# Block 1's mixers: mLSTM decay rows as one product of both parts, scores in single-pass parts with two heads in turns, and k norms taken from the transposed k

## The chip, the cores and the metric

The kernel runs on one core of one Trainium2 chip. The metric is the device time of the program in microseconds (us), the median of several runs.

## The reference, cut to what matters

Two decoder blocks over 512 tokens of width 1024. Block 1 has two mixers side by side on the same normed input: a gated delta rule (GDN, 4 heads, head width 128) and an mLSTM (4 heads, query and key width 64, value width 128). The change touches two places of block 1.

```
qkv  = silu(causal_conv(concat[gq, gk, gv]))     # GDN inputs
k    = gk * rsqrt(sum(gk*gk, -1) + 1e-6)         # the k norm of each token and head
o_a  = gated_delta_rule(q, k, v, g, beta)

# mLSTM, here written over the whole sequence:
d_log[t, s] = b[t] - b[s] + i[s]   for s <= t, else -inf      # b: cumulative log forget gate
s[t, s]     = (q[t] . k[s]) * exp(d_log[t, s] - m[t])          # m: running maximum
num, den    = s @ v, sum(s, -1)
h           = num / max(|den|, exp(-m))
```

Then both mixers' outputs go through head norms, gates and projections; a feed-forward layer and a gate with `p` close block 1. Block 2 has a linear recurrence, a stick-breaking attention with 16 heads of width 64, and two feed-forward layers.

## The kernel before, in words

Everything is in fp32 of high accuracy. A weight matrix or an activation is held as two fp32r parts, `hi` (a rounded copy, written by ScalarE) and `lo` (what is left over, by VectorE: line 102 for weights), and a product is made of three single-pass matmuls (`mm3`, lines 173 to 175): low by high, high by low, high by high. A `slab` is one such projection of 128 output channels by 512 tokens: 24 matmuls of 128x512. It is a generator that yields after 6 matmuls; one such step is called a piece. `todo` holds the slabs of the projections that are still to come, `fill(n)` issues the next n pieces, and `after(n, fn)` has fn called n pieces later (`late`, `run_late`). TensorE's order is the order in which the code is written (`manual_schedule` for PE only); a planner orders the other engines' instructions at build time.

So in block 1 the small products of the two mixers are written between pieces of the large projections. The stretch that matters is the mLSTM loop, lines 586 to 612. For each head h and each 128-row block j of keys (w = 512, 384, 256, 128 query columns remain):

- `psS`: scores k.q, one matmul on fp32 tiles `mkT`, `mqT` (64 partitions: rows 0 to 63 for even heads, 64 to 127 for odd heads). The trace shows it as two instructions.
- `psr`: the row b[t] - m[t] of head h, spread over 128 partitions: two fp32r matmuls of 4 partitions (`sel` with `rjl`, then with `rjh`).
- ScalarE takes exp of `psr` into `D`, GpSimd cuts the triangle (`affine_select`), VectorE multiplies `psS` by `D` into `Sm` (line 601).
- `fill(2)`: two pieces.

After the four j of a head, `psn` (fp32, `Sm` by `mv`, line 608) is made in two groups, each followed by `fill(2)`. A loop over all heads has 48 pieces. `psS`, `psr`, `psn`, `pm` and others rotate in two PSUM banks with the tag "sa"; transposes use two with the tag "sb". The slabs that fill the loop are the 12 of GDN's q, k and v. When a slab ends, VectorE runs its convolution (`conv_silu`: six instructions of 128x512, lines 457 to 464), and six pieces later come its norm sums and transposes. For k that is `l2cols` (`pc`, line 474: four fp32 matmuls with a column of ones, eight instructions in the trace), a power -0.5 on GpSimd (line 203), the transpose `pk`, the multiply into `kn`, and two pieces later the transpose back (`pk2`).

Ahead of the loop, the tag "mvt" (two buffers) holds `zr` (gates, transposed by `pg`, line 391) and then the v projections on their way to their transposes (`pmv`, line 380). The rows are prepared in `rj` and split into `rjh` and `rjl`; `pm` and `enm` make exp(-m) by columns.

Of the kernel before, what the change touches and what calls it, by code (L numbers as in the profile page):

```python
# [9 lines left out]
F32 = mybir.dt.float32  # L10
F32R = mybir.dt.float32r
AF = mybir.ActivationFunctionType
# [41 lines left out]
def block_kernel(ctx: ExitStack, tc: tile.TileContext, xT, pT, cols, cst, wA, wBr, wO, w13, w2, wPG, wPL,  # L54
# [4 lines left out]
    def dump(name, aps):  # L59
        if dbg and name in dbg:  # L60
            for i, a in enumerate(aps):
                nc.sync.dma_start(dbg[name][i], a)
# [15 lines left out]
    def col(name, i=0, n=1):  # L78
        o, c = COFF[name]
        return COL[:, o + i:o + i + n]  # L80
# [115 lines left out]
    def bc_in(ap, n):  # L196
        return ap.unsqueeze(2).to_broadcast([ap.shape[0], ap.shape[1], n])
# [53 lines left out]
    def xtile(k):  # L251
        return xp.tile([P, T], F32, tag=f"x{k}", name=f"x{k}")
# [35 lines left out]
    with ExitStack() as ca:  # L288
# [3 lines left out]
        def pt(name, tag="sa", shape=(P, H, P)):  # L292

            return pps.tile(list(shape), F32, tag=tag, name=name)
# [15 lines left out]
        def after(n, fn):  # L310
            late.append((now[0] + n, fn))
# [9 lines left out]
        def fill(n):  # L321
            for _ in range(n):
                run_late(now[0])
                now[0] += 1
                while todo and next(todo[0], 1):
                    todo.pop(0)
# [15 lines left out]
        psq0 = gemm(pps, wA[O_MQ], A, tag="sb")  # L342
        R = norm_rows(pn, "nr", ss, "R0", rc0)
        LB = ca.enter_context(tc.tile_pool(name="LB", bufs=1, reuse_waits="tile"))
        o_b = LB.tile([P, H, T], F32, name="o_b")
        gz = LB.tile([P, H, T], F32, name="gz")
        cg = ExitStack()
        GP = cg.enter_context(tc.tile_pool(name="GP", bufs=1, reuse_waits="tile"))
# [11 lines left out]
        V.tensor_tensor(zr, psg, R, op=ALU.mult)  # L360
        V.tensor_scalar(zr, zr, col("gbias"), None, op0=ALU.add)

        mkT, mqT = [xtile(0), xtile(1)], [xtile(2), xtile(3)]
        for i in range(2):
            V.tensor_tensor(mkT[i], psk[i], R, op=ALU.mult)
        mv = ML.tile([P, NB, H, P + 1], F32, name="mv")
        G.memset(mv[:, :, :, P:P + 1], 1.0)

        def mq_done(i):
            return lambda ps: V.scalar_tensor_tensor(mqT[i], ps, 0.125, R, op0=ALU.mult, op1=ALU.mult)  # L370

        def mv_done(h):
            def f(ps):
# [77 lines left out]
        cwh = GP.tile([P, 48], F32, name="cwh")  # L451
        V.tensor_scalar(cwh, col("conv", 0, 48), 0.5, None, op0=ALU.mult)

        def conv_silu(ps, ti, out):
            cx = CV.tile([P, T + 3], F32, tag="cx", bufs=2, name="cx")
            G.memset(cx[:, 0:3], 0.0)
            V.tensor_tensor(cx[:, 3:], ps, R, op=ALU.mult)
            ac = CV.tile([P, T], F32, tag="ac", bufs=2, name="ac")
            V.tensor_scalar(ac, cx[:, 0:T], cwh[:, 4 * ti:4 * ti + 1], None, op0=ALU.mult)
            for j in range(1, 4):  # L460
                V.scalar_tensor_tensor(ac, cx[:, j:j + T], cwh[:, 4 * ti + j:4 * ti + j + 1], ac, op0=ALU.mult, op1=ALU.add)
            th = CV.tile([P, T], F32, tag="th", bufs=2, name="th")
            S.activation(th, ac, AF.Tanh)
            V.scalar_tensor_tensor(out, th, 1.0, ac, op0=ALU.add, op1=ALU.mult)

        def l2sq(src):
            sq = CV.tile([P, T], F32, tag="sq", bufs=2, name="sqk")
            S.activation(sq, src, AF.Square)
            return sq

        def l2cols(sq, which, h):
            pc = pn.tile([P, NB], F32, tag="nr", name="pc")
            for b in range(NB):
                TE.matmul(pc[:, b:b + 1], sq[:, b * P:(b + 1) * P], onec, start=True, stop=True)
            r = rqk[:, which, h, :]
            V.tensor_scalar(r, pc, EPS, None, op0=ALU.add)
            pw(r, r)
            return r

        def k_done(h):  # L480
            def f(ps):
                kt = CV.tile([P, T], F32, tag="cv", bufs=3, name="kt")
                conv_silu(ps, 3 * h, kt)
                sq = l2sq(kt)

                def g():
                    rk = l2cols(sq, 0, h)
                    pk = pt("pk", "sb")
                    for b in range(NB):
                        TE.transpose(pk[:, b, :], kt[:, b * P:(b + 1) * P], ident)  # L490
                    V.tensor_tensor(kn[:, :, h, :], pk, bc_in(rk, P), op=ALU.mult)
                    after(2, g2)

                def g2():
                    pk2 = pt("pk2", "sb")
                    for b in range(NB):
                        TE.transpose(pk2[:, b, :], kn[:, b, h, :], ident)
                    S.copy(knT[:, h, :], pk2.rearrange("p b t -> p (b t)"))
                after(LAG, g)
            return f  # L500
# [29 lines left out]
        def mo_done(h):  # L530
            def f(ps):
                assert ob_ready
                th = tp.tile([P, T], F32, tag="xin", bufs=3, name="tho")
                V.tensor_tensor(th, ps, R, op=ALU.mult)
                S.activation(th, th, AF.Tanh, scale=0.5)
                V.tensor_scalar(th, th, 0.5, 0.5, op0=ALU.mult, op1=ALU.add)
                V.tensor_tensor(o_b[:, h, :], o_b[:, h, :], th, op=ALU.mult)
            return f

        LAG = 6  # L540
# [19 lines left out]
        V.tensor_tensor_scan(mrow, rows[:, 0, :], rows[:, 1, :], 0.0, op0=ALU.add, op1=ALU.max)  # L560

        rj = ML.tile([H, 1280], F32, name="rj")
        ro = (0, 512, 896, 1152)
        for j in range(NB):
            V.tensor_tensor(rj[:, ro[j]:ro[j] + P], rows[:, 2, j * P:(j + 1) * P], mrow[:, j * P:(j + 1) * P],
# [2 lines left out]
            V.tensor_scalar(rj[:, ro[j] + P:ro[j + 1]], rj[:, ro[j + 1]:ro[j + 1] + T - (j + 1) * P],  # L568
                            rows[:, 2, (j + 1) * P - 1:(j + 1) * P], None, op0=ALU.add)
        fill(8)  # L570
        sel = ML.tile([H, H], F32R, name="sel")
        V.tensor_copy(sel, ident[0:H, 0:H])
        rjh = ML.tile([H, 1280], F32R, name="rjh")
        S.copy(rjh, rj)
        V.tensor_tensor(rj, rj, rjh.bitcast(F32), op=ALU.subtract)
        rjl = ML.tile([H, 3 * T], F32R, tag="rows", name="rjl")[:, 0:1280]
        V.tensor_copy(rjl, rj)
        pm = pt("pm", shape=(P, NB, H))
        for b in range(NB):
            TE.transpose(pm[:, b, :], mrow[:, b * P:(b + 1) * P], ident[0:H, 0:H])  # L580
# [2 lines left out]
        num = [xtile(4 + b).rearrange("p (h d) -> p h d", h=H) for b in range(NB)]  # L583
        den = ML.tile([P, NB, H], F32, name="den")
        msq = ML.tile([P, NB, H], F32, name="msq")
        for h in range(H):
            p0 = (h % 2) * 64
            Sm = ML.tile([P, 1280], F32, tag="Sm", bufs=1, name="Sm")
            for j in range(NB):
                w = T - j * P  # L590
                psS = pt("psS", shape=(P, T))
                TE.matmul(psS[:, 0:w], mkT[h // 2][p0:p0 + 64, j * P:(j + 1) * P], mqT[h // 2][p0:p0 + 64, j * P:],
                          start=True, stop=True)
                psr = pt("psr", shape=(P, T))
                for n, r_ in enumerate((rjl, rjh)):
                    TE.matmul(psr[:, 0:w], sel[:, h:h + 1].to_broadcast([H, P]), r_[:, ro[j]:ro[j] + w], start=(n == 0), stop=(n == 1))
                D = ML.tile([P, T], F32, tag="D", bufs=2, name="D")
                S.activation(D[:, 0:w], psr[:, 0:w], AF.Exp, bias=ccol[:, j, h:h + 1])
                G.affine_select(D[:, 0:P], D[:, 0:P], pattern=[[1, P]], base=0, channel_multiplier=-1,
                                compare_op=ALU.is_ge, fill=0.0)  # L600
                V.tensor_tensor(Sm[:, ro[j]:ro[j] + w], psS[:, 0:w], D[:, 0:w], op=ALU.mult)
                fill(2)
            for i2 in range(2):
                psn = pt("psn", shape=(P, 2, P + 1))
                for ii in range(2):
                    i = 2 * i2 + ii
                    for j in range(i + 1):
                        TE.matmul(psn[:, ii, :], Sm[:, ro[j] + (i - j) * P:ro[j] + (i - j + 1) * P], mv[:, j, h, :], start=(j == 0), stop=(j == i))
                for ii in range(2):
                    S.copy(num[2 * i2 + ii][:, h, :], psn[:, ii, 0:P])  # L610
                V.tensor_copy(den[:, 2 * i2:2 * i2 + 2, h:h + 1], psn[:, :, P:P + 1])
                fill(2)
        for b in range(NB):
            sqm = ML.tile([P, H, P], F32, tag="D", bufs=2, name="sqm")
            S.activation(sqm, num[b], AF.Square)
            V.tensor_reduce(msq[:, b], sqm, axis=AX.X, op=ALU.add)
        ad = ML.tile([P, NB, H], F32, name="ad")
# [10 lines left out]
        for b in range(NB):  # L628
            V.tensor_tensor(num[b], num[b], bc_in(mz.rearrange("p (b h) -> p b h", h=H)[:, b, :], P), op=ALU.mult)
        def ob_out():  # L630
            for h in range(H):
                po = pt("po", "sb")
                for b in range(NB):
                    TE.transpose(po[:, b, :], num[b][:, h, :], ident)
                S.activation(o_b[:, h, :], po.rearrange("p b t -> p (b t)"), AF.Copy, scale=col("mln", h))
            dump("o_b", [o_b[:, h, :] for h in range(H)])
            ob_ready.append(1)
        fill(LAG)
        run_late(1 << 30)
# [178 lines left out]
        BR = ca.enter_context(tc.tile_pool(name="BR", bufs=1, reuse_waits="tile"))  # L818
        oab = xset(BR, "o")
        for h in range(H):  # L820
            split(oab[4 + h], o_b[:, h, :])
        for h in range(H):
            V.tensor_tensor(oaT[:, h, :], oaT[:, h, :], gz[:, h, :], op=ALU.mult)
            split(oab[h], oaT[:, h, :])
# [579 lines left out]
```

## Time and profile before

| what | value |
|---|---|
| runs, median (lowest to highest) | 2080.22 us (2080.13 to 2083.77), 3 runs |
| the profiled execution's own time | 2082.17 us |
| its span, first to last instruction | 2080.2 us |
| TensorE busy | 2051.9 us, 99% |
| VectorE / ScalarE / GpSimd busy | 53% / 37% / 12% |
| mean granted TensorE clock | 0.995 |

The profiled execution's own time is 2.0 us longer than its span. A change in TensorE's time is to be read as start-to-start distances: matmuls are pipelined, so the durations of single ones overlap and add up to more than the time they take. The chain of waits adds up without overlap.

### The profile page before, as it was taken

What the parts mean: (1) busy time and instruction counts of PE and PEld (TensorE: products, weight loads), DVE (VectorE), ACT (ScalarE), POOL (GpSimd) and SP (SyncE); (2) the same over time, 40 slices, a digit from 0 to 9 for tenths busy, and PEclk for the clock granted to TensorE, in tenths of its full rate; (3) what the DMA queues carried; (4) which work ended last, traced back from release to release, by engine and by line L of the source; (5) the groups of instructions that cost most, each with busy time, mean ns of one, the idle gap of its engine ahead of it and who ended that gap; (6) DMA issues with size and microseconds to landing.
All of it is one profiled execution on the core that took longest, in us unless ns stands there. A gap on an engine that the chain in (4) does not pass through costs nothing.

```text
span 2080.2 us, 24373 instructions
## 1 busy us (share of the span) xinstructions
PE 2051.9 (99%) x9786; PEld 1705.2 (82%) x9786; DVE 1104.5 (53%) x1455; ACT 763.9 (37%) x1099; POOL 257.1 (12%) x266
## 2 busy tenths in 40 slices
PE   8999999999999999999899999999999999999998
PEld 7778899888888888887788888888888888888887
DVE  5667453554444423669964444333877754444322
ACT  4334232333232322546642323223555533322221
POOL 0111000131000000252320000001322220000011
PEclk9999999999999999999999999999999999999999
DMA  4211111343333333322323333333122123333332
GB/s 168 71 55 59 60 41 43 105 127 101 97 96 100 91 97 98 114 79 82 91 91 96 97 101 92 92 101 98 55 61 72 41 77 96 91 102 94 92 102 68
DMA packets 53664, 181.69 MB, mean 87 GB/s; under 512 B 5808, under 2 KB 7984, under 8 KB 53552
## 3 DMA queue, kind: packets, MB, share of 16 engines
q1 hardware_dynamic: 53408, 180.05, 28.9%
q8 instruction: 76, 1.25, 0.3%
q14 instruction: 36, 0.29, 0.0%
q10 hardware_dynamic: 144, 0.10, 0.0%
HBM read 178.03 MB, written 2.10 MB: 87 GB/s over the span
## 4 chain that ended last, share of the span: by engine, by line
PE 91%; DVE 5%; ACT 1%; issue 1%; POOL 1%; DMA 1%; SPq 0%; POOLq 0%; DVEq 0%; ACTq 0%
PE psmm L173 19%; PE psmm L174 19%; PE psmm L175 19%; PE psd L173 6%; PE psd L175 6%; PE psd L174 6%; PE z L1119 2%; PE po L1157 1%; DVE wlo L102 1%; PE pU L731 1%; PE pX L726 1%; PE t L1146 1%; DVE xc L987 1%; PE psv L173 1%; PE psv L174 1%
## 5 line engine op out<-in xcount | busy, mean ns | idle before, releaser
L101 ACT CAST whi<-raw 128x1024 fp32r<-128x1024 f32 (+1 forms) x333 | 344.5, 1036 | 942.3 <-issue 374.5
L102 DVE TENSOR_TENSOR wlo<-raw,whi 128x1024 fp32r<-128x1024 f32 (+1 forms) x333 | 411.0, 1235 | 287.9 <-ACT whi L101 287.8
L173 PE MATMUL psmm<-Bh,wlo 128*128 128x512 f32 x1032 | 402.3, 390 | 0.3 <-DVE Ol L1162 0.3
L174 PE MATMUL psmm<-Bl,whi 128*128 128x512 f32 x1032 | 402.2, 390 | 0.1
L175 PE MATMUL psmm<-Bh,whi 128*128 128x512 f32 x1032 | 402.1, 390 | 0.0
L173 PE MATMUL psmm<-Ah,wlo 128*128 128x512 f32 x832 | 332.9, 401 | 2.8 <-DVE wlo L102 1.9
L175 PE MATMUL psmm<-Ah,whi 128*128 128x512 f32 x832 | 325.2, 391 | 0.0
L174 PE MATMUL psmm<-Al,whi 128*128 128x512 f32 x832 | 324.4, 390 | 0.6 <-DVE Al L189 0.6
L173 PEld LDWEIGHTS psmm<-Bh,wlo 128*128 128x128 f32 x1032 | 193.8, 188 | 40.8 <-DVE Ol L1162 0.5
L175 PEld LDWEIGHTS psmm<-Bh,whi 128*128 128x128 f32 x1032 | 193.8, 188 | 40.3
L174 PEld LDWEIGHTS psmm<-Bl,whi 128*128 128x128 f32 x1032 | 193.8, 188 | 40.2 <-DVE Bl L189 0.5
L216 POOL TENSOR_TENSOR ss<-ss,sq 128x512 f32<-128x512 f32 x55 | 85.6, 1561 | 1141.7 <-issue 803.7
L173 PE MATMUL psd<-Hh,wlo 128*128 128x512 f32 x506 | 196.8, 389 | 0.0
L174 PE MATMUL psd<-Hl,whi 128*128 128x512 f32 x506 | 196.8, 389 | 0.0
L175 PE MATMUL psd<-Hh,whi 128*128 128x512 f32 x506 | 196.8, 389 | 0.0
L173 PEld LDWEIGHTS psmm<-Ah,wlo 128*128 128x128 f32 x832 | 156.3, 188 | 36.0 <-DVE wlo L102 3.2
L175 PEld LDWEIGHTS psmm<-Ah,whi 128*128 128x128 f32 x832 | 156.1, 188 | 33.6
L174 PEld LDWEIGHTS psmm<-Al,whi 128*128 128x128 f32 x832 | 156.6, 188 | 30.3 <-DVE Al L189 1.1
L870 DVE TENSOR_TENSOR u<-psmm,R 128x512 f32<-128x512 f32 x66 | 45.6, 691 | 194.2 <-PE psmm L175 194.2
L866 DVE TENSOR_TENSOR s<-psmm,R 128x512 f32<-128x512 f32 x66 | 45.7, 692 | 137.0 <-PE psmm L175 134.0
L175 PEld LDWEIGHTS psd<-Hh,whi 128*128 128x128 f32 x506 | 95.0, 188 | 19.8
L174 PEld LDWEIGHTS psd<-Hl,whi 128*128 128x128 f32 x506 | 95.0, 188 | 19.8
(468 smaller groups left out, 2475.9 us busy)
## 6 DMA issues: line engine op xcount, KB each, us to landing
raw<-in_f SPq DMA_DIRECT2D x120, 512.0 KB, 3.6
raw<-in_w SPq DMA_DIRECT2D x60, 512.0 KB, 3.5
raw<-in_wA SPq DMA_DIRECT2D x43, 512.0 KB, 3.5
raw<-in_bQKV SPq DMA_DIRECT2D x24, 512.0 KB, 3.5
raw<-in_aIn SPq DMA_DIRECT2D x16, 512.0 KB, 3.6
raw<-in_f SPq DMA_DIRECT2D x16, 384.0 KB, 3.1
x<-in_xT SPq DMA_DIRECT2D x16, 256.0 KB, 3.6
raw<-in_wBr SPq DMA_DIRECT2D x8, 512.0 KB, 3.5
```

The source lines that it names most:

```text
L101: copied[0] = S.copy(hi[:, :nk, :], raw[:, :nk, :])
L102: V.tensor_tensor(lo[:, :nk, :], raw[:, :nk, :], hi[:, :nk, :].bitcast(F32), op=ALU.subtract)
L173: TE.matmul(ps, l, xh, start=(first and i == 0), stop=False)
L174: TE.matmul(ps, h, xl, start=False, stop=False)
L175: TE.matmul(ps, h, xh, start=False, stop=(last and i == n - 1))
L216: eng.tensor_tensor(self.acc, self.acc, sq, op=ALU.add)
L726: heads(lambda h: TE.matmul(pX[:, h], Nm[:, h, :], odd(U)[:, h], start=True, stop=True))
L731: heads(lambda h: TE.matmul(pU[:, h], Tt[:, h, :], X[:, h], start=True, stop=True))
L866: V.tensor_tensor(s1, p1, R, op=ALU.mult)
L870: V.tensor_tensor(u, p3, R, op=ALU.mult)
L987: V.scalar_tensor_tensor(ac, cx[:, j:j + T], col("aconv", 4 * k + j), ac, op0=ALU.mult, op1=ALU.add)
L1119: TE.matmul(zs[g][:, o:o + w], qp[a][qs], kp[b][p0:p0 + 64, 0:w], start=(n == 0 and o == 0), stop=(n == 2), skip_group_check=True)
```

## The change

The mLSTM's k and q become pairs of parts (`mparts`: VectorE scales into a buffer of the tag "mvt", ScalarE and VectorE split it), the low parts in `mlo`, which shares its place with the later `o_b`. The rows' two parts are laid out in one tile `rjp`: partitions 0 to 3 and 64 to 67 hold the high parts, 32 to 35 and 96 to 99 the low parts, zeros elsewhere; `sel2` has the selecting ones at the same places. One matmul of 64 partitions then gives the sum of both parts. The loop goes over two pairs of heads: for each j first the two `psr` (rows 0 to 63 for the even head, 64 to 127 for the odd one), two pieces, then the scores as three single-pass matmuls for each head, the two heads in turns, and two pieces. exp writes straight into `Sm` (now two buffers). All `psn` of a pair follow. For k, `pc` is gone: ScalarE squares the transposed `pk` out of PSUM, VectorE reduces it, and the transpose back comes five pieces later instead of two. The three zeros ahead of each convolution are written once.

```diff
+        def mparts(k, src, c):
+            t = ML.tile([P, T], F32, tag="mvt", bufs=2, name="mkq")
+            V.scalar_tensor_tensor(t, src, c, R, op0=ALU.mult, op1=ALU.mult)
+            pair = xp.tile([P, T], F32R, tag=f"x{k}", name=f"mh{k}"), mlo[:, k, :]
+            split(pair, t)
+            return pair
...
-                sq = l2sq(kt)
                 def g():
-                    rk = l2cols(sq, 0, h)
                     pk = pt("pk", "sb")
                     for b in range(NB):
                         TE.transpose(pk[:, b, :], kt[:, b * P:(b + 1) * P], ident)
+                    sq = CV.tile([P, NB, P], F32, tag="sq", bufs=2, name="sqk")
+                    S.activation(sq, pk, AF.Square)
+                    rk = rqk[:, 0, h, :]
+                    V.tensor_reduce(rk, sq, axis=AX.X, op=ALU.add)
+                    V.tensor_scalar(rk, rk, EPS, None, op0=ALU.add)
+                    pw(rk, rk)
                     V.tensor_tensor(kn[:, :, h, :], pk, bc_in(rk, P), op=ALU.mult)
-                    after(2, g2)
+                    after(5, g2)
...
+        S.copy(rjp[0:H], rj)
+        rj2 = ML.tile([H, 3 * T], F32, tag="rows", name="rj2")[:, 0:1280]
+        V.tensor_tensor(rj2, rj, rjp[0:H].bitcast(F32), op=ALU.subtract)
+        S.copy(rjp[64:64 + H], rj)
+        for c in (32, 96):
+            V.tensor_copy(rjp[c:c + H], rj2)
...
-        for h in range(H):
-            for j in range(NB):
-                psS = pt("psS", shape=(P, T))
-                TE.matmul(psS[:, 0:w], mkT[h // 2][p0:p0 + 64, j * P:(j + 1) * P], mqT[h // 2][p0:p0 + 64, j * P:],
-                          start=True, stop=True)
-                psr = pt("psr", shape=(P, T))
-                for n, r_ in enumerate((rjl, rjh)):
-                    TE.matmul(psr[:, 0:w], sel[:, h:h + 1].to_broadcast([H, P]), r_[:, ro[j]:ro[j] + w], start=(n == 0), stop=(n == 1))
+        for hp in range(2):
+            for j in range(NB):
+                psr = [pt("psr", shape=(P, T)) for _ in range(2)]
+                for c, h in hc:
+                    p0 = 64 * c
+                    TE.matmul(psr[c][:, 0:w], sel2[p0:p0 + 64, h:h + 1].to_broadcast([64, P]),
+                              rjp[p0:p0 + 64, ro[j]:ro[j] + w], start=True, stop=True)
+                Ds = [Sms[h][:, ro[j]:ro[j] + w] for c, h in hc]
+                for c, h in hc:
+                    S.activation(Ds[c], psr[c][:, 0:w], AF.Exp, bias=ccol[:, j, h:h + 1])
+                    G.affine_select(Ds[c][:, 0:P], Ds[c][:, 0:P], pattern=[[1, P]], base=0, channel_multiplier=-1,
+                                    compare_op=ALU.is_ge, fill=0.0)
                 fill(2)
+                psS = [pt("psS", shape=(P, T)) for _ in range(2)]
+                for n, (a, b) in enumerate(((1, 0), (0, 1), (0, 0))):
+                    for c in range(2):
+                        p0 = 64 * c
+                        TE.matmul(psS[c][:, 0:w], kh[a][p0:p0 + 64, j * P:(j + 1) * P], qh[b][p0:p0 + 64, j * P:],
+                                  start=(n == 0), stop=(n == 2))
+                for c in range(2):
+                    V.tensor_tensor(Ds[c], psS[c][:, 0:w], Ds[c], op=ALU.mult)
+                fill(2)
...
-            sqm = ML.tile([P, H, P], F32, tag="D", bufs=2, name="sqm")
+            sqm = ML.tile([P, H, P], F32, tag="D", bufs=1, name="sqm")
```

## Rows read from the trace of the kernel before

**Rows 1.** The page: busy time (us, share, instructions), and the chain's shares.

```profile
PE 2051.9 (99%) x9786; PEld 1705.2 (82%) x9786; DVE 1104.5 (53%) x1455; ACT 763.9 (37%) x1099; POOL 257.1 (12%) x266
...
PE 91%; DVE 5%; ACT 1%; issue 1%; POOL 1%; DMA 1%; SPq 0%; POOLq 0%; DVEq 0%; ACTq 0%
```

**Rows 2.** Stretches: the mLSTM loop, 69 to 171 us: length, busy times, clock.

```profile
69.00:171.00 102.00, 102.00 (x501) 76.34 (x500) 69.71 (x115) 35.87 (x63) 17.51 (x33) 1.00 0.20 58
```

**Rows 3.** Chain of waits, 69 to 171 us: shares by line, pieces (start, length).

```profile
by line: PE psmm L173 22.0%; PE psmm L175 20.0%; PE psmm L174 20.0%; PE psS L592 11.5%; PE psr L596 7.7%; PE psn L608 7.2%; PE pc L474 6.2%; PE pk L490 1.9%; PE pv L517 1.7%; PE pk L497 1.6%; PE pm L580 0.3%
...
69.57 1.05 PE psS L592 x2
70.62 0.66 PE psr L596 x2
```

**Rows 4.** Chain of waits, 81 to 98 us.

```profile
82.31 0.23 PE psmm L175
82.54 0.41 PE psS L592 x2
82.95 0.36 PE psr L596 x2
83.32 0.98 PE pc L474 x8
...
93.02 0.79 PE pc L474 x8
...
96.64 1.05 PE psS L592 x2
```

**Rows 5.** Chain of waits, 1450 to 1456 us: block 2's scores of one head.

```profile
1451.23 2.12 PE z L1119 x12
1453.35 0.43 PE psmm L173
```

**Rows 6.** Timeline of TensorE there: start, duration, line, tile, shape.

```profile
1452.14 0.34 PE L1119 MATMUL z<-kh,ql 64*128 64x384 f32 x1
1452.32 0.34 PE L1119 MATMUL z<-kh,qh 64*128 64x384 f32 x1
...
1452.56 0.27 PE L1119 MATMUL z<-kh,ql 64*128 64x128 f32 x1
1452.67 0.27 PE L1119 MATMUL z<-kh,qh 64*128 64x128 f32 x1
...
1452.95 0.28 PE L1119 MATMUL z<-kh,ql 64*128 64x256 f32 x1
1453.08 0.28 PE L1119 MATMUL z<-kh,qh 64*128 64x256 f32 x1
```

**Rows 7.** Timeline of ScalarE as the loop begins (bracket: idle before, releaser).

```profile
69.31 1.04 ACT L101 CAST whi<-raw 128x1024 fp32r<-128x1024 f32 x1 [2.22 <-PE psmm L175]
70.27 0.18 ACT L582 ACTIVATE enm<-pm 128x16 f32<-128x16 f32 x1
71.32 0.69 ACT L598 ACTIVATE D<-psr,ccol 128x512 f32<-128x512 f32 x1 [0.87 <-PE psr L596]
...
76.13 0.63 ACT L468 ACTIVATE sqk<-kt 128x512 f32<-128x512 f32 x1
```

**Rows 8.** Timeline of VectorE, second head, first key block.

```profile
96.68 0.69 DVE L457 TENSOR_TENSOR cx<-psmm,R 128x512 f32<-128x512 f32 x1 [2.67 <-PE psmm L175]
...
99.88 0.69 DVE L601 TENSOR_TENSOR Sm<-psS,D 128x512 f32<-128x512 f32 x1 [0.19 <-POOL D L599]
100.49 1.53 DVE L461 SCALAR_TENSOR_TENSOR ac<-cx,cwh,ac 128x512 f32<-128x512 f32 x2
```

**Rows 9.** Timelines of VectorE and GpSimd after the loop.

```profile
167.08 1.38 POOL L203 TENSOR_TENSOR rqk<-rqk,mhalf 128x4 f32<-128x4 f32 x1 [0.48 <-DVE rqk L476]
...
177.28 0.63 DVE L616 TENSOR_REDUCE msq<-sqm 128x4 f32<-128x512 f32 x1
```

**Rows 10.** Chain of waits, 30 to 180 us: transposes ahead of the loop.

```profile
36.84 0.44 PE pg L391 x4
...
45.49 0.44 PE pmv L380 x4
```

More of the change, by code (lines that the diff above doesn't have):

```diff
@@ L344, in block_kernel @@
         LB = ca.enter_context(tc.tile_pool(name="LB", bufs=1, reuse_waits="tile"))
-        o_b = LB.tile([P, H, T], F32, name="o_b")
+        mlo = LB.tile([P, 4, T], F32R, tag="ob", name="mlo")
+        o_b = []
         gz = LB.tile([P, H, T], F32, name="gz")
@@ L361, in block_kernel @@
         V.tensor_scalar(zr, zr, col("gbias"), None, op0=ALU.add)
-        mkT, mqT = [xtile(0), xtile(1)], [xtile(2), xtile(3)]
-        for i in range(2):
-            V.tensor_tensor(mkT[i], psk[i], R, op=ALU.mult)
+        def mparts(k, src, c):
[4 more added lines that the diff above has]
+            return pair
+        mkT, mqT = [mparts(i, psk[i], 1.0) for i in range(2)], [None, None]
         mv = ML.tile([P, NB, H, P + 1], F32, name="mv")
@@ L369, in mq_done @@
         def mq_done(i):
-            return lambda ps: V.scalar_tensor_tensor(mqT[i], ps, 0.125, R, op0=ALU.mult, op1=ALU.mult)
+            return lambda ps: mqT.__setitem__(i, mparts(2 + i, ps, 0.125))
         def mv_done(h):
@@ L452, in block_kernel @@
         V.tensor_scalar(cwh, col("conv", 0, 48), 0.5, None, op0=ALU.mult)
+        cxs = [CV.tile([P, T + 3], F32, name=f"cx{i}") for i in range(2)]
+        for cx in cxs:
+            G.memset(cx[:, 0:3], 0.0)
         def conv_silu(ps, ti, out):
-            cx = CV.tile([P, T + 3], F32, tag="cx", bufs=2, name="cx")
-            G.memset(cx[:, 0:3], 0.0)
+            cx = cxs[ti % 2]
             V.tensor_tensor(cx[:, 3:], ps, R, op=ALU.mult)
@@ L536, in f @@
                 V.tensor_scalar(th, th, 0.5, 0.5, op0=ALU.mult, op1=ALU.add)
-                V.tensor_tensor(o_b[:, h, :], o_b[:, h, :], th, op=ALU.mult)
+                V.tensor_tensor(o_b[0][:, h, :], o_b[0][:, h, :], th, op=ALU.mult)
             return f
@@ L562, in block_kernel @@
         rj = ML.tile([H, 1280], F32, name="rj")
+        rjp = ML.tile([P, 1280], F32R, name="rjp")
+        G.memset(rjp.bitcast(F32), 0.0)
+        sel2 = ML.tile([P, H], F32R, name="sel2")
+        V.memset(sel2.bitcast(F32), 0.0)
+        for c in range(0, P, 32):
+            V.tensor_copy(sel2[c:c + H], ident[c:c + H, c:c + H])
         ro = (0, 512, 896, 1152)
@@ L570, in block_kernel @@
         fill(8)
[L571 to L577, printed above, removed]
+        S.copy(rjp[0:H], rj)
[4 more added lines that the diff above has]
+            V.tensor_copy(rjp[c:c + H], rj2)
         pm = pt("pm", shape=(P, NB, H))
@@ L585, in block_kernel @@
         msq = ML.tile([P, NB, H], F32, name="msq")
-        for h in range(H):
-            p0 = (h % 2) * 64
-            Sm = ML.tile([P, 1280], F32, tag="Sm", bufs=1, name="Sm")
+        Sms = [None] * H
+        for hp in range(2):
+            kh, qh = mkT[hp], mqT[hp]
+            hc = [(0, 2 * hp), (1, 2 * hp + 1)]
+            for c, h in hc:
+                Sms[h] = ML.tile([P, 1280], F32, tag="Sm", bufs=2, name="Sm")
             for j in range(NB):
                 w = T - j * P
-                psS = pt("psS", shape=(P, T))
-                TE.matmul(psS[:, 0:w], mkT[h // 2][p0:p0 + 64, j * P:(j + 1) * P], mqT[h // 2][p0:p0 + 64, j * P:],
-                          start=True, stop=True)
-                psr = pt("psr", shape=(P, T))
-                for n, r_ in enumerate((rjl, rjh)):
-                    TE.matmul(psr[:, 0:w], sel[:, h:h + 1].to_broadcast([H, P]), r_[:, ro[j]:ro[j] + w], start=(n == 0), stop=(n == 1))
[L597 to L601, printed above, removed]
-                fill(2)
[L603 to L611, printed above, removed]
-                fill(2)
@@ new lines, in block_kernel @@
+                psr = [pt("psr", shape=(P, T)) for _ in range(2)]
[4 more added lines that the diff above has]
+                Ds = [Sms[h][:, ro[j]:ro[j] + w] for c, h in hc]
+                for c, h in hc:
+                    S.activation(Ds[c], psr[c][:, 0:w], AF.Exp, bias=ccol[:, j, h:h + 1])
+                    G.affine_select(Ds[c][:, 0:P], Ds[c][:, 0:P], pattern=[[1, P]], base=0, channel_multiplier=-1,
+                                    compare_op=ALU.is_ge, fill=0.0)
@@ new lines, in block_kernel @@
+                fill(2)
+            for h in (2 * hp, 2 * hp + 1):
+                for i2 in range(2):
+                    psn = pt("psn", shape=(P, 2, P + 1))
+                    for ii in range(2):
+                        i = 2 * i2 + ii
+                        for j in range(i + 1):
+                            TE.matmul(psn[:, ii, :], Sms[h][:, ro[j] + (i - j) * P:ro[j] + (i - j + 1) * P], mv[:, j, h, :], start=(j == 0), stop=(j == i))
+                    for ii in range(2):
+                        S.copy(num[2 * i2 + ii][:, h, :], psn[:, ii, 0:P])
+                    V.tensor_copy(den[:, 2 * i2:2 * i2 + 2, h:h + 1], psn[:, :, P:P + 1])
+                    fill(2)
@@ L630, in ob_out @@
         def ob_out():
+            o_b.append(LB.tile([P, H, T], F32, tag="ob", name="o_b"))
             for h in range(H):
@@ L634, in ob_out @@
                     TE.transpose(po[:, b, :], num[b][:, h, :], ident)
-                S.activation(o_b[:, h, :], po.rearrange("p b t -> p (b t)"), AF.Copy, scale=col("mln", h))
-            dump("o_b", [o_b[:, h, :] for h in range(H)])
+                S.activation(o_b[0][:, h, :], po.rearrange("p b t -> p (b t)"), AF.Copy, scale=col("mln", h))
+            dump("o_b", [o_b[0][:, h, :] for h in range(H)])
             ob_ready.append(1)
@@ L820, in block_kernel @@
         for h in range(H):
-            split(oab[4 + h], o_b[:, h, :])
+            split(oab[4 + h], o_b[0][:, h, :])
         for h in range(H):
```

## The prediction

> **What bounds the kernel now.** I read the page first: TensorE is busy for 99% of the span and carries 91% of the chain that ended last, while no other engine is over 53% [rows 1]. So a microsecond taken from TensorE is a microsecond of the kernel, unless TensorE then has to wait. Next the stretches: in the mLSTM loop, 69 to 171 us, TensorE is busy for 102.00 of 102 us at the full granted clock, VectorE for 69.71, ScalarE for 35.87 and GpSimd for 17.51 [rows 2]. There is no gap to fill; only shorter TensorE work helps. Then the chain of waits, whose pieces add up without overlap: it tells what each small product costs between the large ones [rows 3, 4]. Last, block 2's scores, because they are what the new scores look like: 64 partitions, fp32r, three passes [rows 5, 6].
>
> **What leaves TensorE.** psS holds 11.5% of the 102 us, 11.7 us, and psr 7.7%, 7.9 us [rows 3]. The matmul behind such a group is also longer: the first large one after block 2's scores takes 0.43 instead of 0.23 us [rows 4, 5], and pc takes 0.98 behind a psr but 0.79 elsewhere [rows 4]. With 0.19 for each of the 16 groups that is 3.0 us more. Together 11.7 + 7.9 + 3.0 = 22.6 us for scores and rows. The four k norms lose their pc, at 0.79 each (the 0.19 is already counted): 3.2 us. psn, the transposes and the 48 pieces stay.
>
> **What comes in its place.** Every j of a pair of heads has one group of two psr and one of six score matmuls, so 2 x 4 x 2 = 16 groups again, and 2 x 4 x 8 = 64 single-pass matmuls. Their prices are in block 2. In a stream, one takes 0.18 us at 384 columns, 0.13 at 256 and 0.11 at 128, by the distances of the starts [rows 6], and 0.23 at 512, as the large ones do [rows 4]. Three of each are 1.95 us. The whole group, with what the next matmul loses, took 2.12 + 0.20 = 2.32 us [rows 5], so going into a group of 64 partitions and out again costs 0.37 us. Sixteen groups: 5.9 us.
>
> What no row shows is how two neighbours on different halves of the partitions go together. Both ends:
> - One after the other: 16 matmuls of each width, 16 x 0.65 = 10.4 us. With the 5.9, 16.3 us; 6.3 us saved.
> - Entirely side by side: half of it, 5.2 us, in all 11.1; 11.5 us saved.
>
> Between them: the 128-column step doesn't halve from 256 to 128 columns (0.13 to 0.11), so something that doesn't depend on the columns holds it; I take that to be the loading of its weights. If the columns of a pair run side by side but the two loads go in line, a pair takes 0.23, 0.22, 0.22 and 0.22 us, four pairs in each of eight j: 4 x 2 x 0.89 = 7.1 us, in all 13.0; 9.6 us saved. I take this. Block 2's matmuls can't overlap, since they share rows and accumulate in one bank; the new neighbours share neither. What speaks against it: psS of an odd head (rows 64 to 127) is as long ahead of its psr (rows 0 to 3) as that of an even head, 1.05 us both times [rows 3, 4], so different rows alone don't make those overlap. But those two have different sizes of row part, and a pair has the same.
>
> The Trainium skill (TensorE: Matmul & The Clock Gate, Part 3) says that matmuls on different row groups of the array run at the same time, a few ns apart; by it alone the saving would be near the 11.5 us, and no run here shows it yet.
>
> **Waits that come new.** The first psr now stands ahead of the first psS, and the pair wants both "sa" banks at once. One is held by pm until enm has read it, and enm stood behind a weight cast on ScalarE until 70.45 us [rows 7]. Before, psS ran meanwhile, from 69.57 to 70.62 [rows 3]; that cover is gone. The second psr could start near 69.9, so I price one wait at 0.6 us.
>
> In the loop each pair waits for the pair before it to leave the two banks, with 12 large matmuls, 12 x 0.23 = 2.8 us, as cover. The scores wait for two exps, 2 x 0.69 = 1.4 us, with a weight cast of 1.04 ahead of them [rows 7]: 2.4 us, which fits. The next psr wait for two multiplies, 2 x 0.69 = 1.4 us at 512 columns, behind the convolution that starts when a slab ends, that is, with the psr. It ran from 96.68 to 102.02 us, one multiply included [rows 8], so 4.7 us without it. The multiplies then end 4.7 + 1.4 = 6.1 us after psr began, and the next pair wants the banks after 0.5 (psr) + 2.8 + 0.9 (scores) + 2.8 = 7.0 us. It fits by 0.9 us, so nothing is charged. If another VectorE instruction of 0.69 or so is planned ahead of the multiplies, it still fits; with two, it doesn't. As the bound above I take 0.27 us at each of the 16 groups, 4.3 us: half of such a late instruction, less what is left of the cover.
>
> **Edits that I cost at nothing, and their cover.** The k norm's new line is Square 0.63 [rows 7], reduce 0.63, power 1.38 [rows 9] and multiply 0.69, some 3.5 us with the small add; five pieces are 5 x 6 x 0.23 = 6.9 us, so pk2 finds kn. With the old two pieces, 2.8 us, it would have waited about 0.7 us for each head. The splits of k and q (a scaling, a copy and a subtraction of about 0.7 us each, four times) pass through two "mvt" buffers, one of which zr keeps until pg, at 36.84. The next thing that TensorE wants from there is pmv at 45.49 [rows 10]: 8.6 us for three sequences of about 2 us. If this cover were short, pmv would wait, by about 1 us. The rows' layout adds a copy on ScalarE and a cast on VectorE ahead of the loop, where both have gaps. sqm has one buffer instead of two, and its squares and reductions take turns; the transposes that want the result come 11 pieces after the last psn, 15 us. The zeros of the convolution free GpSimd alone.
>
> **The sum.** 9.6 + 3.2 - 0.6 = 12.2 us. The profiled execution took 2082.17 us (span 2080.2), so 2070.0 for the like of it. The median of the runs, 2080.22, lies 1.95 below that execution, so 2068.0 us is the forecast.
>
> **Rivals.**
> - *In line:* the halves don't overlap. 6.3 + 3.2 - 0.6 = 8.9 us, 2071.3 us. For it: nothing in this trace shows two matmuls sharing time. Against: rows, banks and weights of the pair are apart.
> - *Banks:* the pairs double what must leave PSUM at once, and a group waits. With 0.27 us at each group on top of the forecast 2072.3 us, on top of the in-line case 2075.6. For it: VectorE is at 68% of the loop [rows 2] and gets a shorter loop with four more reductions. Against: the 0.9 us worked out above. The Trainium skill (TensorEngine Tiling (Array Packing), Performance Considerations, "PSUM Bottleneck") warns of just this: tiling makes TensorE faster, not the emptying of PSUM. By it the gain of the overlap could be lost here; in the trace of before VectorE's 69.71 us fit in 102.
> - *Slower:* the multiplies come so late that each of the eight psr pairs waits. At 2.05 us each, 16.4 us, the gain is gone and 4.2 us more: 2084.4 us. It decides when a whole convolution, 4.7 us, is planned between the scores and their multiplies, so that these end about 2.0 us after the 2.8 us of cover. Against: the multiply of before was let in between the convolution's instructions [rows 8].
> - *No change:* waits of about 12 us in all, or pieces that wait ahead of the loop: 2080 us.
>
> **How the numbers follow.** Chances: forecast (with full overlap at its lower end) 0.50, in line 0.25, banks 0.15, no change 0.06, slower 0.04. The range goes down to full overlap, 2066.1, less 1.6 if the second load of a pair covers 0.1 us of each group's entry: 2064.5. It goes up to in line with waits, 2075.5. That holds the first three cases but for their edges. A measurement here can tell about 0.2%, 4.2 us, from no change; the first three cases lie beyond it, but part of the third could end within: faster 0.88, same 0.08, slower 0.04.
>
> **What would show it.** In the chain of the profile after: psS and psr together, with the longer matmuls behind them, near 13 us in place of 22.6 (16 if in line); starts of the two psr of a pair under 0.2 us apart at 512 columns (0.3 if in line); k's pc gone, q's still there; one wait for enm, and none for D or Sm. The loop would last some 90 instead of 102 us. Wrong it would be if TensorE's waits list the multiplies or exps, or if a group costs much more than 0.37 us to enter and leave.

## The result, and the profile after

Four runs of each kernel, side by side: 2068.99 us median (2068.42 to 2071.58) against 2080.43 us (2080.13 to 2083.77). The ratio is 0.9944, 95% interval 0.9927 to 0.9961: 11.6 us faster, between 8 and 15. The forecast was 2068.0 us, with a range of 2064.5 to 2075.5. The profiled execution took 2071.58 us, with a span of 2069.8.

The page after, busy time, and the stretch of the loop (start and end, length, then busy time of TensorE, its weight loads, VectorE, ScalarE and GpSimd, clock, DMA):

```profile
PE 2037.0 (98%) x9754; PEld 1696.2 (82%) x9754; DVE 1110.8 (54%) x1468; ACT 766.6 (37%) x1104; POOL 261.2 (13%) x257
...
70.00:161.00 91.00, 88.33 (x467) 68.72 (x467) 70.82 (x117) 34.87 (x66) 18.55 (x22) 1.00 0.23 68
```

TensorE still bounds the kernel, but in the loop it is no longer busy throughout: 2.7 of the 91 us are idle, where there was none in [rows 2]. The chain of waits after, the second pair of heads at 512 and 384 columns and the first pair at 128:

```profile
119.91 0.42 PE psr L620 x2
120.33 0.43 PE psmm L173
...
123.28 0.89 PE psS L632 x6
127.53 0.37 PE psr L620 x2
...
130.83 0.72 PE psS L632 x6
```

```profile
95.56 0.26 PE psr L620 x2
95.82 0.43 PE psmm L173
...
98.81 0.48 PE psS L632 x6
```

They answer to [rows 3, 4]. Six score products of 512 columns take 0.89 us, less than the 1.05 of one fp32 product for one head before, and two psr take 0.42 instead of 0.66 for one. The 0.20 that the next matmul loses is as before.

TensorE's waits in the first 200 us (waiter, whom it waited for, total, times, longest):

```profile
PE psg L332 <- ACT whi L273: 5.4, 1, 5.4
PE pk L512 <- DVE kn L506: 2.2, 2, 1.1
PE prow L572 <- ACT rows L573: 0.8, 1, 0.8
PE psmm L173 <- DVE wlo L102: 0.7, 1, 0.7
PE psr L620 <- ACT enm L604: 0.5, 1, 0.5
PE po L670 <- ACT o_b L671: 0.5, 1, 0.5
```

psg, prow and po (0.3 us) waited before too. New are enm, 0.5 us, which was priced at 0.6, and kn, 2.2 us, which was priced at nothing: the transpose back of k found no kn for two of the four heads. The 0.7 us for a weight part (wlo) is new as well, but the control below doesn't have it.

From the end of pm to the end of the last psn, by TensorE's timeline, it was 69.57 to 175.49 us before and 70.56 to 164.59 after: 105.9 and 94.0 us, 11.9 less. The spans differ by 10.4, since the loop began 1.0 us later and some waits outside it differ by a microsecond or two (weight parts: 4.4 us in all against 2.5). The later start isn't the change's doing: in every other trace here pm begins 0.8 to 1.6 us later than in the one trace of before, also with the k norm alone (69.99 against 69.16 us), where TensorE's work ahead of the loop is that of before.

### The profile page after: what moved, and what is told of

Its sections match the earlier page's. It is cut to its first block, busy times and chain, and to the rows that moved or that the text cites. A ratio compares the mean times of both kernels' runs of the same rounds, so it can differ in the third digit from the quotient of the medians.

```text
span 2069.8 us, 24311 instructions
## 1 busy us (share of the span) xinstructions
PE 2037.0 (98%) x9754; PEld 1696.2 (82%) x9754; DVE 1110.8 (54%) x1468; ACT 766.6 (37%) x1104; POOL 261.2 (13%) x257
## 4 chain that ended last, share of the span: by engine, by line
PE 90%; DVE 5%; issue 1%; ACT 1%; POOL 1%; DMA 1%; SPq 0%; POOLq 0%; DVEq 0%; ACTq 0%
PE psmm L173 19%; PE psmm L174 19%; PE psmm L175 19%; PE psd L173 6%; PE psd L175 6%; PE psd L174 6%; PE z L1155 2%; PE po L1193 1%; DVE wlo L102 1%; PE pU L767 1%; PE pX L762 1%; PE t L1182 1%; DVE xc L1023 1%; PE psv L173 1%; PE psv L174 1%
```

## Experiments

Each ratio is to runs of the kernel before on the same chip and in the same job, five runs of each experiment unless said otherwise. Differences between experiments are differences of these ratios, with 0.0010 as 2.1 us. One ratio's interval reaches some 2.7 us to either side, a difference of two some 4 us, so for small differences the traces decide, and each experiment has one trace.

**The change again**, as a control beside the second set.

> The changed kernel itself once more, beside the three others of this job: 2069 us within the scatter, with the two waits for kn (2.2 us) and the one for enm (0.5 us) in the list again if they belong to the program and not to one execution.

Measured: 2069.74 us (2068.61 to 2071.39, 5 runs), ratio 0.9944 (0.9930 to 0.9958). kn 2.2 and enm 0.5 us are in the list again. The 0.7 us for a weight part is not: that one belonged to one execution. The profiled execution's span was 2067.0 us, 2.8 less than the first one's.

**Heads apart**: are the halves side by side at all? The comments in the cut sum up the lines that they stand for.

```diff
-        for hp in range(2):
+        for h in range(H):
+            hp, p0 = h // 2, 64 * (h % 2)
             for j in range(NB):
-                # two psr, fill(2), six score products in turns, two multiplies, fill(2)
+                # one psr, three score products (rows p0 to p0 + 63), one multiply, fill(2)
```

> The changed kernel with the heads one after another instead of in pairs: for each head and j one row product and three score products, all four on the same half of the partitions, then two pieces. As many groups (16) and as many matmuls (64), but no neighbour on the other half. Theory (the halves run side by side in the change): the 64 matmuls take 4 x 4 x 0.65 = 10.4 us plus 5.9 for going in and out, 16.3 us against about 11.1 in the change, so 5.2 us slower, 2074.2 us. Rival (order and pairing don't matter, single-pass parts give all): 2069.0 us.

Measured: 2071.97 us, ratio 0.9954 (0.9942 to 0.9967), 2.1 us slower than the change. Its chain, second head, 512 and 384 columns:

```profile
95.94 0.43 PE psr L616
96.37 0.69 PE psS L620 x3
...
100.02 0.37 PE psr L616
100.39 0.53 PE psS L620 x3
```

One psr for one head costs 0.43 us, as much as the two for a pair in the change; three score products cost 0.69 against six in 0.89, of which some 0.2 is the way in. Over all widths (psr 0.43, 0.37, 0.31, 0.26; scores 0.69, 0.53, 0.36, 0.33) four heads take 13.1 us; the change's two pairs take 2 x 4.00 = 8.0. So by the trace the pairs save 5.1 us of TensorE work, where the theory said 5.2, and "in line" is refuted. The time shows less, since in this order kn was never waited for (2.2 us back); a difference of 2.1 us alone would decide nothing.

**No turns**: does the order within the group matter?

```diff
                 for c, h in hc:
-                    p0 = 64 * c
+                    p0 = 0                    # both psr on the lower half
...
-                for n, (a, b) in enumerate(((1, 0), (0, 1), (0, 0))):
-                    for c in range(2):
+                for c in range(2):
+                    for n, (a, b) in enumerate(((1, 0), (0, 1), (0, 0))):
```

> The changed kernel with the pairs taken apart: both row products on the lower 64 partitions, and the three score products of one head before those of the other. Same instructions, same count. Theory (neighbours on different halves run side by side, loads included): each group of six scores keeps only one overlap, where one head follows the other, so it grows by two matmul steps, 0.46 us at 512 columns (0.89 to about 1.35 in the chain), and each pair of rows by one step (0.42 to about 0.65); 3 x 0.65 x 2 = 3.9 us in all, about 2072.9 us. Rival (halves never overlap, the saving is only that of single-pass parts and one row product): no change, 2069.0 us.

Measured: 2071.01 us, ratio 0.9952 (0.9940 to 0.9965), 1.7 us slower. The psr part came as expected, the scores did not. Timeline of TensorE and then the chain, 512 columns:

```profile
75.46 0.51 PE L632 MATMUL psS<-mh,mlo 64*128 64x512 f32 x2
75.80 0.41 PE L632 MATMUL psS<-mlo,mh 64*128 64x512 f32 x2
76.02 0.41 PE L632 MATMUL psS<-mh,mh 64*128 64x512 f32 x2
```

```profile
120.89 0.66 PE psr L620 x2
124.51 0.91 PE psS L632 x6
```

Two psr on one half take 0.66 instead of 0.42 us: one step of 0.23 more, so they go one after the other (0.54 for 0.37 at 384, 0.36 for 0.26 at 128). But the six scores, written as three of one head and then three of the other, still take 0.91 us, and the timeline shows them start two by two. The other head's first product, fourth in the code, started with the first. That the queue holds them in the order of the code, the semaphore counts in the trace bear out: in turns the last product of the second head adds a single count at each of the eight places, while here the last products of both heads add several at once. So what matters is that the group holds work for both halves; the turns themselves gave nothing. The theory's 1.3 us for psr was right, its 2.6 us for the scores wrong.

**The old k norm**, with the rest of the change.

```diff
+                sq = l2sq(kt)
...
+                    rk = l2cols(sq, 0, h)
...
-                    S.activation(sq, pk, AF.Square)
...
-                    V.tensor_reduce(rk, sq, axis=AX.X, op=ALU.add)
...
-                    after(5, g2)
+                    after(2, g2)
```

> The changed kernel with the k norm as before: squares from the untransposed k, four products with a column of ones, the transpose back two pieces later. Theory (the new k norm saves 3.2 us of TensorE work but made the transpose back wait twice for 1.1 us): those two waits go and 3.2 us of products come back, so about 1.0 us slower, 2070.0 us. Rival (the transposes' waits are only taken from a later wait): 3.2 us slower, 2072.2 us.

Measured: 2069.72 us, ratio 0.9945 (0.9932 to 0.9957): 0.2 us slower, which tells little by itself. No wait for kn is in its trace and no other has taken its place, so by the trace the new norm in this place was worth 3.2 - 2.2 = 1.0 us.

**The k norm alone**, put into the kernel before.

```diff
 # before.py
-                    rk = l2cols(sq, 0, h)
...
+                    S.activation(sq, pk, AF.Square)
...
+                    V.tensor_reduce(rk, sq, axis=AX.X, op=ALU.add)
...
-                    after(2, g2)
+                    after(5, g2)
```

> The kernel before with the new k norm alone (transpose back five pieces later), scores and rows as before. Theory: the products with ones are gone, 3.2 us, and the line of about 10 us finds five pieces and the groups between them, some 9 to 10 us: between no wait and 1.1 us for each head, so 2077.2 to 2081 us, nearer the lower end. Rival (the norm is worth its 3.2 us in full): 2077.2 us with no wait for kn.

Measured: 2076.89 us (9 runs), ratio 0.9980 (0.9971 to 0.9990), 4.2 us faster than before (2.1 to 6.0), and no wait for kn: the rival's case. So it is not the norm's line by itself that is too long for five pieces, but that line in the new order of the loop. The timelines of ScalarE and VectorE for the first head show another order on both engines: the Square stands ahead of the weight cast and the reduction ahead of the weight's low part.

```profile
86.41 0.58 ACT L490 ACTIVATE sqk<-pk 128x512 f32<-128x512 f32 x1
87.53 1.05 ACT L101 CAST whi<-raw 128x1024 fp32r<-128x1024 f32 x1 [0.54 <-PE psmm L175]
```

```profile
88.14 0.67 DVE L492 TENSOR_REDUCE rqk<-sqk 128x4 f32<-128x512 f32 x1
...
89.20 1.22 DVE L102 TENSOR_TENSOR wlo<-raw,whi 128x1024 fp32r<-128x1024 f32 x1
...
91.32 0.69 DVE L495 TENSOR_TENSOR kn<-pk,rqk 128x512 f32<-128x512 f32 x1 [0.17 <-POOL rqk L203]
```

From the end of pk's transposes (84.73) kn took 7.3 us here, and the transposes back came 2.6 us after it (94.57).

**Two pieces** instead of five.

```diff
-                    after(5, g2)
+                    after(2, g2)
```

> The changed kernel with k's transpose back two pieces after the norm, as before the change. Theory (the norm's line takes about 10 us): three pieces less are 4.1 us less cover; in the trace of the change two heads waited 1.1 us and the other two had about 2 us to spare, so the waits become 2 x 5.2 + 2 x 2.1 = 14.6 us instead of 2.2: 12.4 us slower, 2081.4 us. Rival (the prediction's 3.5 us line): a wait of 0.7 us for each head, 2.8 instead of 2.2, 2069.6 us.

Measured: 2099.05 us (4 runs), ratio 1.0084 (1.0070 to 1.0097), some 29 us slower than the change. The waits, the stretches behind each of the four (start and end, length, busy times, granted clock, DMA), and the chain behind the first wait:

```profile
PE pk L512 <- DVE kn L506: 22.4, 4, 6.5
```

```profile
93.12:96.20 3.08, 3.08 (x10) 2.60 (x11) 0.54 (x1) 0.59 (x1) 0.00 (x0) 0.50 0.00 0
123.50:126.92 3.42, 3.42 (x10) 2.63 (x9) 0.69 (x1) 1.10 (x2) 0.00 (x0) 0.50 0.03 13
154.95:161.05 6.10, 6.10 (x16) 4.52 (x16) 0.45 (x1) 0.59 (x1) 0.00 (x0) 0.50 0.00 0
186.37:191.77 5.40, 5.40 (x15) 4.43 (x16) 1.88 (x3) 1.10 (x2) 0.00 (x0) 0.50 0.04 17
```

```profile
93.12 1.11 PE pk L512 x4
94.24 0.43 PE psmm L173
...
95.94 0.41 PE psmm L174
96.35 0.23 PE psmm L175
```

All four heads waited, 22.4 us in all, 20.2 more than in the change. I had taken off 4.1 us of cover for the three pieces alone; but the small products between the pieces went with them, and by the timelines the cover fell from 9.1 to 3.1 us for the first head and from 9.9 to 3.5 for the second. The other 9 us are in the clock. TensorE waited 6.4, 4.6, 6.5 and 4.9 us, and then worked at half the full clock (0.50, that is 1.2 instead of 2.4 GHz) for 18.0 us in the four stretches together. The large matmuls take 0.43 us there, and are back at 0.23 from 96.35 on; an estimate from these numbers: at 0.23 for 0.43 the 18.0 us of work would take 8.4 us less, at double the clock 9.0. The rival, the 0.7 us for each head of the prediction, is refuted.

**Seven pieces.**

```diff
-                    after(5, g2)
+                    after(7, g2)
```

> The changed kernel with the transpose back of k seven pieces later instead of five. Theory (k's norm line needs about 10 us, since its Square is queued behind a weight cast and its reduction behind the convolution; two pieces are 2.8 us more): no wait of TensorE for kn, 2.2 us faster, 2066.8 us. Rival (the wait moves to the next user of the same PSUM banks or to the loop's end): no change, 2069.0 us.

Measured: 2066.34 us, ratio 0.9931 (0.9917 to 0.9944), 2.7 us faster than the change by the ratios, which is within their scatter of some 4 us; its slowest run, 2068.16, is below the change's fastest, 2068.42, but that ran in another job. The trace decides: no wait for kn is left, and it did not move elsewhere. Its chain also has the groups of 256 columns, which the change's chain leaves out:

```profile
133.88 0.31 PE psr L620 x2
137.16 0.55 PE psS L632 x6
```

**Seven pieces and two more covers.**

```diff
-                    after(5, g2)
+                    after(7, g2)
...
-            V.tensor_copy(sel2[c:c + H], ident[c:c + H, c:c + H])
+            G.tensor_copy(sel2[c:c + H], ident[c:c + H, c:c + H])
...
-        pm = pt("pm", shape=(P, NB, H))
+        pm = pt("pm", "sb", shape=(P, NB, H))
```

> As the one with seven pieces, and two more covers: the tile pm in the other pair of PSUM banks, so that the first pair of rows needn't wait for enm, and the four selecting copies on GpSimd instead of VectorE, where they stood ahead of a weight split at the kernel's start. Theory: 0.5 us and up to 0.7 us less than the seven pieces alone, about 2065.6 us, with neither wait in the list. Rival (these waits are of one execution only, or covered by others): 2066.8 us.

Measured: 2065.38 us (2064.35 to 2067.92), ratio 0.9925 (0.9913 to 0.9938): 4.0 us faster than the change and the fastest version here. The first psr now follow pm at once:

```profile
70.32 0.34 PE pm L602 x4
70.65 0.42 PE psr L620
```

enm is gone from the list. The step from the seven pieces, 1.2 us by the ratios, is smaller than the interval; by the trace 0.5 us of it are enm's. What the copies on GpSimd gave can't be told, since the weight wait that they were to remove was absent from the control as well.

## Why the prediction was right, and where it was right by chance

- *What bounds it, and what leaves TensorE.* Right. The kernel followed TensorE's work, and pc's 3.2 us came in full where nothing waited (the k norm alone: 4.2 us, interval 2.1 to 6.0).
- *Sixteen groups at 0.37 us for the way in and out.* Right. psr and psS take 2 x (0.42 + 0.37 + 0.31 + 0.26 + 0.89 + 0.72 + 0.55 + 0.48) = 8.0 us, with 16 x 0.19 behind them 11.0 us, 11.6 less than the 22.6 of before. The lower bound, everything side by side, was 11.1; the sign looked for was near 13.
- *The weight loads of a pair go in line.* This step failed: I took 7.1 us for the products where the bound below, 5.2, was the true one. At 128 columns the two psr take 0.26 us and three pairs of scores 0.48, so a further pair costs 0.11 us, what [rows 6] have for one matmul: the loads cost no more in a pair than alone. 13.0 - 11.0 = 2.0 us were missed here. The Trainium skill (TensorE: Matmul & The Clock Gate, Part 3) says that matmuls on different row groups run at the same time, and the trace agrees: six products in 0.89 us. It also says that matmuls start in the order of the program; what the last section reports differs from that.
- *In line.* Refuted by the heads apart: 13.1 against 8.0 us.
- *enm.* Right: 0.5 us for 0.6, and gone when pm has other banks.
- *Banks, and slower.* No wait for D, Sm or a bank of theirs in any trace of the change. The 0.9 us that were left held: for the second pair at 512 columns the multiplies ended 5.9 us after psr began (6.1 in the prediction), and the next psr came 7.6 us after it (7.0). The 0.27 us for each group doesn't follow from the prediction's own words, since one instruction of 0.69 fits into 0.9. The warning of the Trainium skill (TensorEngine Tiling (Array Packing), Performance Considerations), that tiling doesn't speed up the emptying of PSUM, did not come true for these banks; VectorE's two multiplies, which empty them, do stand in the k norm's line below, with 0.75 us.
- *The k norm at nothing, five pieces as cover.* This step failed, by 2.2 us. I added durations, 3.5 us, and left out what stands ahead of each on its engine; the line took 10.1 us for two heads and 8.0 and 8.3 for the others. The cover was misjudged too, the other way: 9.1 us instead of 6.9 for the first head (83.39 to 92.47), since two psr, six scores and q's pc stand between the five pieces. The chain of the change shows the line for the first head, from the end of pk's transposes at 83.39 us to the transposes back:

```profile
82.80 0.59 PE pk L499 x4
...
86.23 1.06 ACT whi L101
...
87.32 1.23 DVE wlo L102
88.54 0.66 DVE ac L472
89.21 0.60 DVE rqk L503
89.81 0.24 DVE ac L472
...
90.38 0.75 DVE Sm L635 x2
91.13 0.09 DVE rqk L504
...
91.29 1.45 POOL rqk L203
...
92.77 0.70 DVE kn L506
...
93.51 0.66 PE pk L512 x4
```

  The reduction, the add, the power and kn are 2.8 us of these 10; the rest is a weight's two parts, the convolution of the next slab and the multiplies of the two heads, on the engines' queues ahead of it. ScalarE's timeline says why the Square was late:

```profile
84.62 0.63 ACT L474 ACTIVATE th<-ac 128x512 f32<-128x512 f32 x1 [3.76 <-DVE ac L472]
86.23 1.05 ACT L101 CAST whi<-raw 128x1024 fp32r<-128x1024 f32 x1 [0.98 <-PE psmm L175]
87.19 0.63 ACT L479 ACTIVATE sqk<-qT 128x512 f32<-128x512 f32 x1
87.72 0.59 ACT L501 ACTIVATE sqk<-pk 128x512 f32<-128x512 f32 x1
```

  pk was there at 83.4. ScalarE stood idle until 84.62, waiting for the convolution, and for 0.98 us more for a weight buffer, while the Square stood fourth in its queue. Yet the Square ended at 88.31 and the reduction began only at 89.2: VectorE had the weight's low part, which waited for the same cast, and a step of the convolution in front of it. So it is the order on both engines. Two, five and seven pieces gave 22.4, 2.2 and 0 us of wait. Two other kernels here have the same norm and five pieces with the reduction ahead of the weight's low part, the k norm alone and the heads apart: kn came 7.3 to 7.7 us after pk in both, with 2.2 to 2.6 us to spare, and no head waited. Both also differ in the loop's groups; a kernel that changes nothing but the order on these engines wasn't tried.
- *The sum.* 11.6 + 3.2 - 0.5 - 2.2 = 12.1 us is what the traces' terms give (11.9 from pm to the last psn, 11.6 by the ratio), and 9.6 + 3.2 - 0.6 = 12.2 was forecast. The two failed steps, 2.0 us too little and 2.2 too much, cancelled: that the forecast came so close was luck.

## What to carry to other kernels

Products that use half of TensorE's partitions are worth pairing with the other half: a second one of the same width cost nothing here. When a chain of small instructions on other engines is given a cover, don't sum their durations but count what is queued ahead of them on each engine, and give a piece or two more, since a miss stalls the bounding engine and can slow its clock too. A first use that hides a wait (psS ahead of psr) is a cover as well; look what it hid before moving it.

## What the hardware showed that I had not expected

TensorE took matmuls on different halves out of the order of the code: with three products for one half written ahead of three for the other, the fourth started with the first, and the six took 0.91 us, against 0.89 us in turns. On the same half they stayed in line (two psr: 0.66 instead of 0.42 us). And 22.4 us of waits, 6.5 at most, cost 29 us: 20.2 as waits beyond those of the change, and some 9 because behind each wait TensorE ran at half the full clock (0.50) for 3.1 to 6.1 us.
